# Two-layer hybrid trunk in fp32: wide GpSimd steps of layer 0, ple_proj and the gates moved to VectorE and ScalarE, gate inputs deferred by one half, ScalarE's table load moved ahead

## The chip, the cores and the metric

The kernel runs on one core of one Trainium2 chip. Its time is the device time of one execution in microseconds: 2993.09 us before, the median of 3 runs (2991.86 to 2994.93). One execution was profiled; it took 2989.8 us, and its span, from the first to the last record, is 2988.1 us.

## The reference

Two layers on 1024 tokens of 1024 features, all in fp32. Layer 0 mixes tokens by RWKV-7 (8 heads of 64) and by gated DeltaNet (4 heads of 128) side by side, layer 1 by softmax attention over bands of chunks. What both layers do around their mixer:

```python
for i in range(DEPTH):                       # DEPTH = 2
    h = rmsnorm(x, norm_mix_g[i])
    if i % 2 == 0:
        proj = h @ even_w_in[e]
        dh = token_shift(h) - h
        y_a, v_first = rwkv7_group(h, dh, ...)        # uses (h + dh*mu) @ w1 and the like: the LoRA products
        y_b = gdn_group(...)
        mix = jnp.concatenate([y_a, y_b], -1) @ even_w_out[e]
    else:
        mix = chunk_band_attention(h, attn_w_qkv[o], ...) @ attn_w_out[o]
    x = x + mix
    hf = rmsnorm(x, norm_ffn_g[i])
    x = x + jnp.square(jax.nn.relu(hf @ mlp_w1[i])) @ mlp_w2[i]
    x = x + rmsnorm(p[i] @ ple_w_proj[i], ple_norm_g[i]) * jax.nn.sigmoid(x @ ple_w_gate[i])
return x
```

The last line is the gated embedding. Its first factor needs only `p`, the second needs x after the MLP.

## The kernel before

Tensors lie with features on the 128 partitions and tokens along the row, in tiles of 128 x 512: eight feature tiles, each with two token halves (`hf`). Every fp32 product is three passes on TensorE: ScalarE rounds an operand to a high part (`whi`, or the first half of `xg`, `act`), VectorE subtracts it to get the low part (`wlo`), and high x high, high x low and low x high are summed in a PSUM bank (`mm3`, whose matmuls all carry line 180). `split_w` (L316 and L317) does this for weights, `split_scaled` (L362/363, or L365/366 with a norm's gain) for activations. Weights arrive by SyncE's queue (SP), are split, and are used once.

RMSNorm scales rows, so it is applied behind the products: squares are summed over the eight tiles into `acc`, `row_stats` (L388 and the small steps L294 to L304) sums that over partitions by one-column matmuls and takes the inverse root, `to_rows` spreads it over partitions, and each eviction multiplies by it.

*Order.* Lanes (Python generators for the RWKV heads, the DeltaNet heads, the projections, ple_proj and the first products of the out-projection) are interleaved by a planner, `run`, which takes the lane whose estimated time is smallest. Tile's scheduler then orders each engine's instructions anew by a simulated time line. So an edit in one place can move instructions of other engines nearby.

*The start* (`l0_in`, L591 on). The first x tiles come half by half: two by ScalarE's queue, the others by SP's (L610). Each is split and its squares taken on ScalarE (`square`, L688), and GpSimd adds them to `acc` (L690) for the first token half; for the second half VectorE does. The statistics wait for the eighth: `self.plan` runs `row_stats` when the second projected tile is done and `to_rows` at the third. `lora` (L711) multiplies raw LoRA weights by per-feature mixing factors on GpSimd (L722), splits the two results, and adds the two products on GpSimd (L732). In layer 0 GpSimd also does the triangular solver's small subtractions (L421 to L431, L461), and the solver (`iz`, `F`, `T`, `Z` tiles) copies on ScalarE.

*ple_proj* (L1720). For each of 8 feature tiles and 2 halves: 6 matmuls of p with the embedding's weights, an eviction times `hpleg` (half of the norm's gain, one number per partition) on VectorE (L1740), the square on ScalarE (L1742), its sum on GpSimd (L1744), and a store of the scaled tile to DRAM (`pnd`, L1745). At the end `row_stats`. In layer 0 it lies beside the last units of the mixer (753 to 807 us), in layer 1 beside the last attention heads (2125 to 2172 us). There ScalarE also scales queries and keys (L2006, L2008), takes the softmax's exponentials (L2073) and splits probabilities (L362).

*The gates* (`tail`, L1676 on). Eight output tiles with two halves each. A half is 24 matmuls (`dense`); then, in `ev_gate`: tanh on ScalarE into a scratch tile of a ring of four (L1680), the load of `pn` from DRAM (L1682), its multiplication by the row statistics `prs` on GpSimd (L1683), (tanh + 1) * pn on VectorE (L1684), x += that (L1685), and the store of x (L1687 or L1689). In layer 0 the new x is at once made layer 1's input: split (L1692), squared on ScalarE into another scratch tile (L1695), summed on GpSimd (L1696).

*The seam.* At the last gate tile `load_qkv` (L1917) loads and splits head pair 0's weights `wq` in places of old ring tiles. `attn_in` (L1925) then makes queries, keys and values of four blocks of 128 tokens per half, each in a PSUM bank of 24 matmuls of 128 x 384, which ScalarE (L1946, L1950) and VectorE (L1951) evict with the row factor `rscol`. Blocks 0 and 1 of pair 0 take the two banks `sn`, the others the two of the common ring:

```python
if pr == 0 and i < 2:
    ps = psm.tile([P, HB], F32, tag="sn", name="dps", bufs=2)[...]
else:
    ps = self.bank([P, 3, P])
```

## Time and profile before

| | |
|---|---|
| median of the runs | 2993.09 us (2991.86 to 2994.93) |
| profiled execution | 2989.8 us, span 2988.1 us |
| mean granted TensorE clock | 0.987 |
| busy: TensorE | 2917.3 us (98%) |
| busy: VectorE | 2100.8 us (70%) |
| busy: ScalarE | 1441.8 us (48%) |
| busy: GpSimd | 476.2 us (16%) |
| HBM | 283.54 MB read, 125.89 MB written, 137 GB/s |
| first gate eviction of layer 0 to its last | 1578 to 1659 us |

In the rows of the trace PE is TensorE's matmuls, PEld its weight loads, DVE VectorE, ACT ScalarE, POOL GpSimd, and SPq SyncE's queue of DMA issues. A timeline row gives start, duration, engine, line, operation, output<-input, type and count, and in brackets the idle time of that engine just before and what ended it. Rows such as "L1740 DVE ... 737/748/751" give the shortest, median and longest duration in ns of a group. The granted clock is TensorE's, 1.00 at full speed.

### The profile page before, as it was taken

Reading aid. Unit: us, or ns where it says so; the run is one execution under the profiler, and the core shown is the slowest. Engines: PE = TensorE matmul, PEld = TensorE weight load, DVE = VectorE, ACT = ScalarE, POOL = GpSimd, SP = SyncE. Lnnn points to the kernel's source line nnn. Section 1 sums busy time; section 2 is a strip of 40 time slices with the busy share of each in tenths; the row PEclk is TensorE's granted clock in tenths of the full one; section 3 lists DMA queues with packets and bytes.
Section 4 is the critical chain, followed back from the end, with each engine's and each line's share of the span. In section 5 each row is a group of like instructions: output and inputs, shape, how many; then the busy total and the mean of one; then the engine's idle time right before and its main releaser. Section 6 shows DMA issues by size and latency. Waiting matters only on the chain.

```text
span 2988.1 us, 46702 instructions
## 1 busy us (share of the span) xinstructions
PE 2917.3 (98%) x17190; PEld 2420.8 (81%) x17190; DVE 2100.8 (70%) x4137; ACT 1441.8 (48%) x2828; POOL 476.2 (16%) x947
## 2 busy tenths in 40 slices
PE   8999999999999999999999899999999999999999
PEld 6777778777777888888888899999888888888887
DVE  7665654645749777787886677676859677878883
ACT  4443432323427555544443466666747555544441
POOL 5442330433400000000004211111200000000002
PEclk9999999899999999999999999999999999999999
DMA  6534324232446444754433211110366444754423
GB/s 220 201 127 140 116 86 140 77 120 82 144 141 230 161 149 153 252 179 153 154 111 120 86 49 44 48 63 24 113 234 214 141 155 153 254 182 147 148 97 118
DMA packets 205157, 412.49 MB, mean 138 GB/s; under 512 B 46352, under 2 KB 48640, under 8 KB 204928
## 3 DMA queue, kind: packets, MB, share of 16 engines
q1 hardware_dynamic: 174112, 353.40, 35.8%
q10 hardware_dynamic: 30816, 56.11, 4.9%
q8 instruction: 135, 2.21, 0.3%
q14 instruction: 94, 0.77, 0.1%
HBM read 283.54 MB, written 125.89 MB: 137 GB/s over the span
## 4 chain that ended last, share of the span: by engine, by line
PE 78%; DVE 8%; DMA 6%; POOL 3%; ACT 3%; issue 2%; SPq 0%; ACTq 0%; POOLq 0%; DVEq 0%
PE dps L180 64%; PE ch L180 2%; PE po L180 2%; PE iz L180 1%; PE pt L195 1%; PE pm L180 1%; POOL subt L428 1%; POOL sub L430 1%; PE sn L180 1%; PE tp L180 1%; DVE act L1319 1%; PE py L180 1%; DMA late<-hd 1%; DMA Xp<-z 1%; PE pp L180 1%
## 5 line engine op out<-in xcount | busy, mean ns | idle before, releaser
L180 PE MATMUL dps<-r,act 128*128 128x512 f32 x3720 | 872.3, 392 | 0.4 <-DVE act L1319 0.4
L180 PEld LDWEIGHTS dps<-r,act 128*128 128x128 f32 x3720 | 698.5, 188 | 154.2 <-DVE act L1319 0.9
L180 PE MATMUL dps<-xg,whi 128*128 128x512 f32 x1248 | 419.1, 415 | 13.4 <-ACT whi L316 9.6
L180 PE MATMUL dps<-wq,act 128*128 128x384 f32 x1536 | 303.7, 342 | 8.6 <-ACT late L1680 4.3
L1683 POOL TENSOR_TENSOR pn<-pn,prs 128x512 f32<-128x512 f32 x32 | 45.7, 1431 | 1539.9 <-DVE xw L1586 713.3
L180 PEld LDWEIGHTS dps<-xg,whi 128*128 128x128 f32 x1248 | 227.3, 193 | 63.6 <-ACT whi L316 11.2
L180 PEld LDWEIGHTS dps<-wq,act 128*128 128x128 f32 x1536 | 264.8, 190 | 11.7 <-DVE vs L1951 4.8
L180 PE MATMUL dps<-xg,wlo 128*128 128x512 f32 x624 | 251.5, 404 | 4.6 <-DVE wlo L317 4.6
L1318 ACT CAST act<-act 128x512 fp32r<-128x512 f32 (+2 forms) x281 | 160.4, 600 | 150.3 <-PE dps L180 72.8
L1319 DVE TENSOR_TENSOR act<-act 128x512 fp32r<-128x512 f32 (+2 forms) x281 | 180.7, 670 | 6.7 <-ACT act L1318 6.5
L1318 ACT CAST act<-late 128x512 fp32r<-128x512 f32 x210 | 123.6, 620 | 110.3 <-PE dps L180 94.5
L180 PE MATMUL dps<-act 128*128 128x512 f32 x720 | 175.0, 391 | 1.5 <-DVE late L1440 1.5
L180 PE MATMUL dps<-late,act 128*128 128x512 f32 x672 | 166.7, 393 | 0.0
L1319 DVE TENSOR_TENSOR act<-late,act 128x512 fp32r<-128x512 f32 x210 | 138.7, 685 | 37.5 <-ACT act L1318 37.5
L180 PEld LDWEIGHTS dps<-act 128*128 128x128 f32 x720 | 134.9, 188 | 31.5 <-DVE late L1440 2.3
L180 PEld LDWEIGHTS dps<-late,act 128*128 128x128 f32 x672 | 126.0, 188 | 27.7
L180 PEld LDWEIGHTS dps<-xg,wlo 128*128 128x128 f32 x624 | 120.1, 193 | 34.2 <-DVE wlo L317 7.1
L180 PE MATMUL dps<-xw,act 128*128 128x512 f32 x576 | 145.9, 392 | 1.3 <-ACT act L1318 1.3
L1586 DVE TENSOR_TENSOR xw<-xw,dps 128x512 f32<-128x512 f32 x192 | 129.6, 679 | 21.6 <-PE dps L180 21.6
L180 PEld LDWEIGHTS dps<-xw,act 128*128 128x128 f32 x576 | 107.9, 188 | 25.4 <-ACT act L1318 1.7
L2073 ACT ACTIVATE pb<-pb,mx 128x640 f32<-128x640 f32 (+4 forms) x128 | 89.2, 697 | 51.8 <-DVE mx L2067 50.8
L180 PE MATMUL po<-ptile,vs 128*128 128x256 f32 (+1 forms) x576 | 98.5, 283 | 3.8 <-ACT ptile L362 1.4
(513 smaller groups left out, 5292.6 us busy)
## 6 DMA issues: line engine op xcount, KB each, us to landing
hb<-late ACTq DMA_DIRECT2D x196, 256.0 KB
act<-hb SPq DMA_DIRECT2D x158, 256.0 KB
late<-in_w SPq DMA_DIRECT2D x60, 512.0 KB
act<-in_w SPq DMA_DIRECT2D x112, 256.0 KB
braw<-hb SPq DMA_DIRECT2D x80, 256.0 KB
wd<-whi SPq DMA_DIRECT2D x28, 512.0 KB
wd<-wlo SPq DMA_DIRECT2D x28, 512.0 KB
whi<-wd SPq DMA_DIRECT2D x28, 512.0 KB
```

Of the source, the lines that this page charges most:

```text
L180: return self.begin(self.nc.tensor.matmul(out, lhsT, rhs, start=start, stop=stop, skip_group_check=again))
L195: return self.begin(self.nc.tensor.transpose(out, in_, ident))
L428: E.tensor_tensor(o, X[:, 0:i, i:i + 1].broadcast_to((NP, i, n)), Bq[:, i:i + 1, i + 1:16].broadcast_to((NP, i, n)), op=ALU.mult)
L430: E.tensor_tensor(X[:, 0:i, i + 1:16], X[:, 0:i, i + 1:16], o, op=ALU.add)
L1318: A.copy(hi, s)
L1319: V.tensor_tensor(lo, s, hi.bitcast(F32), op=ALU.subtract)
L1586: V.tensor_tensor(x[n][:, hs[hf]], x[n][:, hs[hf]], ps, op=ALU.add)
L1683: G.tensor_tensor(pn, pn, prs[:, sl], op=ALU.mult)
L2073: A.activation(S, S, AF.Exp, bias=mx[:, 1:2] if nf else mx[:, 0:1], scale=-1.0, accum_out=l)
```

## The change

1. Behind the second x load on ScalarE's queue a Tanh of one column of a constant tile is issued (`early`); the table that ScalarE needs is loaded for it.
2. The first half's square sums go from GpSimd to VectorE, and are written into the plan step of the second projected tile (`first_rows`), with `row_stats`.
3. `lora`: the 12 multiplications of raw weights and the 4 additions go from GpSimd to VectorE.
4. Gates, both layers: `pn` is loaded one half ahead (`load_ple`; the first before the gate loop) and multiplied by `prs` on VectorE at the end of a half's eviction, for the next half (`scale_ple`): 32 multiplications. In layer 0 the making of layer 1's input moves to `next_input`, which is called one half later (at the last tile at once), and its 14 sums go from GpSimd to VectorE.
5. `ple_proj`, both layers: the 32 evictions times `hpleg` go from VectorE to ScalarE, the 28 sums of squares from GpSimd to VectorE.
6. `attn_in`, pair 0: block 3 takes the bank `sf` of its own.

In all 97 wide operations leave GpSimd (952 instructions to 855), VectorE gets these 97 and gives 32, ScalarE gets 32 and the one-column Tanh; TensorE's matmuls and SP's DMAs are the same in number.

```diff
                         (nc.sync if k > 1 else nc.scalar).dma_start(out=xr, in_=a["x"][k, :, 0:HB])
+                        if k == 1:
+                            early = self.sm.tile([P, 4], F32, tag="rsc", name="early")
+                            nc.scalar.activation(early[:, 0:1], self.ones[:, 0:1], AF.Tanh)
...
-                        squares.append(lambda k=k, xr=xr: self.square(acc, xr, k == 0))
-                for f in squares:
-                    f()
+                        squares.append(lambda k=k, xr=xr: self.square(acc, xr, k == 0, nc.vector))
+                def first_rows():
+                    for f in squares:
+                        f()
+                    self.row_stats([acc], rsc)
...
-                    self.late, self.plan = [], {2: lambda: self.row_stats([acc], rsc), 3: ...}
+                    self.late, self.plan = [], {2: first_rows, 3: ...}
...
-                nc.gpsimd.tensor_tensor(wv[:, :, c0:c1], rv[:, :, c0:c1],
+                nc.vector.tensor_tensor(wv[:, :, c0:c1], rv[:, :, c0:c1],
...
-        nc.gpsimd.tensor_tensor(out, out, sb[:, 0:HB], op=ALU.add)
+        nc.vector.tensor_tensor(out, out, sb[:, 0:HB], op=ALU.add)
...
+            def load_ple():
+                if ple:
+                    n, hf = ple.pop(0)
+                    nc.sync.dma_start(out=pn2[:, hf], in_=self.pnd[n][:, hf, :])
+                    landed.append(hf)
+            def scale_ple():
+                if landed:
+                    hf = landed.pop(0)
+                    V.tensor_tensor(pn2[:, hf], pn2[:, hf], prs[:, hs[hf]], op=ALU.mult)
+            def next_input(n, hf):
+                sl = hs[hf]
+                if hf == 0:
+                    xg.append(place(F32R, tag="b" if n < 2 else "a"))
+                self.split_scaled(xg[n], x[n][:, sl], self.vec("mixg", 8 + n), sl)
+                if n:
+                    sq = scr()
+                    A.activation(sq, x[n][:, sl], AF.Square)
+                    V.tensor_tensor(accs[hf], accs[hf], sq, op=ALU.add)
+                else:
+                    A.activation(accs[hf], x[n][:, sl], AF.Square)
...
                     A.activation(sg, ps, AF.Tanh, scale=0.5)
-                    pn = pn2[:, hf]
-                    nc.sync.dma_start(out=pn, in_=self.pnd[n][:, hf, :])
-                    G.tensor_tensor(pn, pn, prs[:, sl], op=ALU.mult)
-                    V.scalar_tensor_tensor(sg, sg, 1.0, pn, op0=ALU.add, op1=ALU.mult)
+                    load_ple()
+                    V.scalar_tensor_tensor(sg, sg, 1.0, pn2[:, hf], op0=ALU.add, op1=ALU.mult)
                     V.tensor_tensor(x[n][:, sl], x[n][:, sl], sg, op=ALU.add)
...
+                    nc.sync.dma_start(out=a["out"][n, :, sl] if last else self.xd[n][:, sl], in_=x[n][:, sl])
+                    if not last:
+                        todo.append((n, hf))
+                        while len(todo) > (n < NK - 1):
+                            next_input(*todo.pop(0))
+                    scale_ple()
...
-                    nc.vector.tensor_scalar(t[:, hf, :], ps, self.dv["hpleg"][:, 8 * i + n:8 * i + n + 1], None, op0=ALU.mult)
+                    nc.scalar.activation(t[:, hf, :], ps, AF.Copy, scale=self.dv["hpleg"][:, 8 * i + n:8 * i + n + 1])
...
-                        nc.gpsimd.tensor_tensor(acc[:, hf, :], acc[:, hf, :], sq, op=ALU.add)
+                        nc.vector.tensor_tensor(acc[:, hf, :], acc[:, hf, :], sq, op=ALU.add)
...
-            if pr == 0 and i < 2:
-                ps = psm.tile([P, HB], F32, tag="sn", name="dps", bufs=2)[:, 0:3 * P].rearrange("p (a c) -> p a c", a=3)
+            if pr == 0 and i in (0, 1, 3):
+                tag, n = ("sn", 2) if i < 2 else ("sf", 1)
+                ps = psm.tile([P, HB], F32, tag=tag, name="dps", bufs=n)[:, 0:3 * P].rearrange("p (a c) -> p a c", a=3)
```

How the order moves is shown at three places. First VectorE at the kernel's start, before; `xg` is the split of x (L366), `wlo` a weight's low part, `ms` and `rsc` the row statistics:

```order
L366 SCALAR_TENSOR_TENSOR xg<-f,vecs,xg 128x512
L317 TENSOR_TENSOR wlo<-wraw,whi 128x512
L366 SCALAR_TENSOR_TENSOR xg<-f,vecs,xg 128x512 x6
L317 TENSOR_TENSOR wlo<-wraw,whi 128x1024 x2
L317 TENSOR_TENSOR wa_434<-wraw,wa_434 128x512
L388 TENSOR_SCALAR ms<-st 128x4
```

and the same place now, where lines carry the changed kernel's numbers (L695 is the sum of squares):

```order
L366 SCALAR_TENSOR_TENSOR xg<-f,vecs,xg 128x512 x2
L695 TENSOR_TENSOR acc<-acc,f 128x512
L366 SCALAR_TENSOR_TENSOR xg<-f,vecs,xg 128x512 x2
L695 TENSOR_TENSOR acc<-acc,f 128x512
L366 SCALAR_TENSOR_TENSOR xg<-f,vecs,xg 128x512
L695 TENSOR_TENSOR acc<-acc,f 128x512
L317 TENSOR_TENSOR wlo<-wraw,whi 128x1024
L695 TENSOR_TENSOR acc<-acc,f 128x512 x3
L317 TENSOR_TENSOR wlo<-wraw,whi 128x1024
L388 TENSOR_SCALAR ms<-st 128x4
```

The seven sums stand between the splits and the wide low parts: four ahead of the first wide `wlo`, three between the two, and the statistics follow directly.

Second VectorE at the last gates of layer 0, before; `late` is the scratch tile, `x` the residual tile, `act` its split, `wq` the attention's weights:

```order
L1684 SCALAR_TENSOR_TENSOR late<-late,pn 128x512
L1685 TENSOR_TENSOR x_12747<-x_12747,late 128x512
L366 SCALAR_TENSOR_TENSOR act<-x_12747,vecs,act 128x512
L1922 TENSOR_TENSOR wq_15706<-late,wq_15705 128x1024
L1684 SCALAR_TENSOR_TENSOR late<-late,pn 128x512
L1685 TENSOR_TENSOR x_12747<-x_12747,late 128x512
L366 SCALAR_TENSOR_TENSOR act<-x_12747,vecs,act 128x512
L1684 SCALAR_TENSOR_TENSOR late<-late,pn 128x512
```

and now (L1713 and L1714 are the gate's two steps, L1693 the scaling of `pn`, L1703 the sum of squares, L1946 the weights' split):

```order
L1713 SCALAR_TENSOR_TENSOR late<-late,pn 128x512
L1714 TENSOR_TENSOR x_12749<-x_12749,late 128x512
L366 SCALAR_TENSOR_TENSOR act<-x_12749,vecs,act 128x512
L1693 TENSOR_TENSOR pn<-pn,prs 128x512
L1703 TENSOR_TENSOR acc<-acc,late 128x512
L1946 TENSOR_TENSOR wq_15706<-late,wq_15705 128x1024
L1713 SCALAR_TENSOR_TENSOR late<-late,pn 128x512
L1714 TENSOR_TENSOR x_12749<-x_12749,late 128x512
L366 SCALAR_TENSOR_TENSOR act<-x_12749,vecs,act 128x512
```

Two steps join each half, the scaling and the sum. The names don't tell the halves of a tile apart, so the rows can't show whose split it is; it stands where it stood, behind the gate's two steps, and the weights' split ahead of the last three halves, as before.

Third ScalarE in ple_proj(1), before; `sq` is the square, `pb` are attention scores, `yr` and `pt` tiles that are split:

```order
L2076 ACTIVATE pb<-pb,rl 128x640
L2073 ACTIVATE pb,rl<-pb,mx 128x640
L1742 ACTIVATE sq<-dps 128x512
L2073 ACTIVATE pb,rl<-pb,mx 128x640
L2076 ACTIVATE pb<-pb,rl 128x640
L362 CAST act<-yr 128x512 x4
L2076 ACTIVATE pb<-pb,rl 128x640
L1742 ACTIVATE sq<-dps 128x512
```

and now (L1764 is the eviction times `hpleg`, L1766 the square, L2098 and L2101 the exponentials and their scaling):

```order
L1764 ACTIVATE act<-dps,d_hpleg 128x512
L2098 ACTIVATE pb,rl<-pb,mx 128x640
L1766 ACTIVATE sq<-dps 128x512
L2098 ACTIVATE pb,rl<-pb,mx 128x640
L1764 ACTIVATE act<-dps,d_hpleg 128x512
L362 CAST act<-yr 128x512 x4
L2101 ACTIVATE pb<-pb,rl 128x640
L1766 ACTIVATE sq<-dps 128x512
L2101 ACTIVATE pb<-pb,rl 128x640
L1764 ACTIVATE act<-dps,d_hpleg 128x512
```

The evictions stand among the exponentials, and a bank's two readers are now both on ScalarE, with other work between them.

19 lines of the change are left out of this document (5 added, 14 removed).

## The prediction

> **What bounds the kernel now.** I read the page's busy times first, then TensorE's waits, then a table of stages, and only then the timelines of the places that the change touches. The executed profile took 2989.8 us, 2988.1 of it span; the runs' median is 2993.09, so 3.3 us more. I make the sum against the profile and put the difference on the median.
>
> ```profile
> PE 2917.3 (98%) x17190; PEld 2420.8 (81%) x17190; DVE 2100.8 (70%) x4137; ACT 1441.8 (48%) x2828; POOL 476.2 (16%) x947
> ```
>
> TensorE is busy 2917.3 of 2988.1 us: 71 us is all that any other engine can give back as waits, and no matmul is removed. TensorE's waits by releaser (us in total, times, longest) tell who holds it:
>
> ```profile
> PE dps L180 <- ACT whi L316: 9.6, 5, 7.1
> PE dps L180 <- ACT late L1680: 4.3, 1, 4.3
> PE dps L180 <- DVE vs L1951: 3.7, 3, 2.2
> ```
>
> The first is mostly the start (7.1, the first matmul), the second and third are the seam between layer 0's gates and layer 1's first qkv products: all in the change's reach. A busy TensorE can also be a slow one. In the table by stages the columns are window, its length, busy time (and count) of PE, PEld, DVE, ACT, POOL, granted clock, DMA share, GB/s:
>
> ```profile
> 0.00:30.00 30.00, 21.08 (x85) 16.16 (x86) 14.25 (x26) 16.43 (x27) 23.15 (x85) 1.00 0.82 301
> 30.00:70.00 40.00, 36.96 (x166) 27.11 (x165) 34.61 (x73) 18.68 (x31) 14.87 (x18) 1.00 0.51 172
> 414.60:418.00 3.40, 3.40 (x19) 2.42 (x19) 2.58 (x8) 1.26 (x3) 1.34 (x5) 0.51 0.38 122
> 421.40:432.00 10.60, 9.98 (x49) 6.83 (x49) 4.87 (x9) 2.03 (x4) 5.87 (x14) 0.52 0.47 135
> 745.00:805.00 60.00, 55.70 (x504) 42.22 (x502) 50.68 (x105) 28.68 (x66) 30.14 (x43) 1.00 0.36 129
> 807.00:821.00 14.00, 13.45 (x60) 10.02 (x55) 8.28 (x21) 4.99 (x9) 3.79 (x10) 0.51 0.64 204
> 1650.20:1657.20 7.00, 5.28 (x17) 5.28 (x18) 4.83 (x5) 3.39 (x6) 3.95 (x3) 0.51 0.24 87
> 2124.00:2172.00 48.00, 44.31 (x269) 37.52 (x267) 43.70 (x115) 42.02 (x89) 20.23 (x15) 1.00 0.43 160
> ```
>
> Four rows stand at half clock. The stretch after the gates follows a wait of TensorE; those at 414.6 and 807 do not: TensorE is busy 3.40 of 3.40 and 13.45 of 14.00 us there, on the delta rule's small products. What half clock costs is half of its length: 7 us at half clock lose 3.5.
>
> **The start** (ScalarE's table, the squares' sums). Rows of ScalarE, GpSimd, VectorE and TensorE:
>
> ```profile
> 3.98 1.28 ACT L365 ACT_TABLE_LOAD   x1 [3.98 <-DMA vecs<-in_vecs]
> 7.13 1.22 PE L180 MATMUL dps<-xg,whi 128*128 128x512 f32 x2 [7.13 <-ACT whi L316]
> 8.39 0.72 ACT L365 ACTIVATE xg<-f,vecs 128x512 fp32r<-128x512 f32 x1 [0.17 <-DMA f<-in_x]
> 13.23 5.76 POOL L690 TENSOR_TENSOR acc<-acc,f 128x512 f32<-128x512 f32 x3
> 15.74 2.09 DVE L317 TENSOR_TENSOR wlo<-wraw,whi 128x1024 fp32r<-128x1024 f32 x1
> 17.89 0.50 PE L180 MATMUL dps<-xg,wlo 128*128 128x512 f32 x1 [1.03 <-DVE wlo L317]
> 422.00 1.23 DVE L317 TENSOR_TENSOR wlo<-wraw,whi 128x1024 fp32r<-128x1024 f32 x1 [3.15 <-ACT whi L316]
> L690 DVE TENSOR_TENSOR acc<-acc,xr x7: 671/680/830, 32.5 to 42.3; 128x512 f32<-128x512 f32 x7
> ```
>
> The table load waits for the vectors until 3.98, and takes 1.28. The early Tanh reads only a constant, so the load runs while ScalarE idles, and the first split, the first weight cast and the first matmul come up to 1.28 us earlier. But the third x tile lands at about 8.3 either way (the 8.39 row): of the 1.28 I count 0.7, with ends 0 and 1.28. The seven sums go from GpSimd (5.76/3 = 1.92 each) to VectorE (0.68). Beside GpSimd a wlo took 2.09, against the 1.23 that a 128x1024 wlo takes at 422.00, with GpSimd idle: 0.86 of the 1.03 wait at 17.89 goes. Against it, 7 x 0.68 = 4.8 us now stand in VectorE's own order, four sums among the splits and three, 2.0 us, between the two wide wlo's; it has 14.25 of 30 us busy and the splits wait for tiles, so I let the gaps hide them. I take **-1.5** for the start. Ends: -3 (both effects whole, and the statistics earlier) and +2 (the three sums, 2.0 us, in front of a wlo that is waited for).
>
> **The LoRA multiplies and adds.** In 30 to 70 us VectorE is 34.61 of 40 busy, so the eight 128x512 multiplies are not free there; what they buy is rows like these:
>
> ```profile
> 51.44 1.29 POOL L732 TENSOR_TENSOR f<-f,raw 128x512 f32<-128x512 f32 x1
> 51.56 1.20 DVE L783 TENSOR_SCALAR gs_ab<-gs_ab 128x16 f32<-128x16 f32 x1
> 53.01 0.17 DVE L783 TENSOR_SCALAR gs_ab<-gs_ab 128x16 f32<-128x16 f32 x1
> 54.58 0.50 PE L180 MATMUL dps<-xg,wlo 128*128 128x512 f32 x1 [0.98 <-DVE wlo L317]
> 418.99 1.89 POOL L722 TENSOR_TENSOR wraw<-lraw,d_omul 128x1024 f32<-128x1024 f32 x1 [1.97 <-DMA lraw<-in_lora]
> 422.02 1.22 PE L180 MATMUL dps<-xg,whi 128*128 128x512 f32 x2 [1.16 <-ACT whi L316]
> ```
>
> The 16-element operation beside the GpSimd add takes 1.20 in place of 0.17, and the wlo behind it is late by that 1.03; the add itself on VectorE costs 0.68, so 0.35 is won at such a place and 0.68 lost where nothing was stretched. First half: **-0.5**, ends -2 and +2 (four wide places each way). At 419 the multiply of 1.89 stands in TensorE's way (the 1.16 wait); on VectorE it takes about 1.23, a wlo's size, and 0.7 goes. The half clock from 421.4 may begin one 3.4 us grain later or not: **-1.0**, ends -4 and +1.
>
> **ple_proj(0).** VectorE gives 16 evictions and takes 14 adds; GpSimd gives the adds:
>
> ```profile
> L1740 DVE TENSOR_SCALAR xg<-dps,d_hpleg x16: 737/748/751, 753.5 to 800.9; 128x512 f32<-128x512 f32 x16
> L1744 POOL TENSOR_TENSOR xg<-xg,xs x14: 1249/1273/1717, 760.6 to 804.3; 128x512 f32<-128x512 f32 x14
> 787.40 1.67 DVE L297 TENSOR_TENSOR rsw<-fr 128x4 f32<-128x4 f32 x1
> 790.63 0.62 PE L195 MATMUL pp<-ident,fr 128*128 128x128 f32 x4 [1.35 <-DVE fr L304]
> 805.57 1.05 PE L180 MATMUL dps<-ones,xg 128*128 128x1 f32 x8 [0.47 <-POOL xg L1744]
> ```
>
> VectorE, 50.68 of 60, sheds 16 x 0.748 - 14 x 0.68 = 2.4 us, and its 4-element steps (1.67 here) are no longer stretched, so the 1.35 wait goes. ScalarE, 28.68 of 60, has room for 16 evictions. The last statistics come 1.27 - 0.68 = 0.6 earlier plus whatever queued on GpSimd. The half clock that follows (13.6 us, from 807) may shrink by one grain of 3.4, worth 1.7. I take 1.35 + 1.7 = **-3.0**. Ends: -8 (the stretch gone as well) and +2 (ScalarE's longer evictions in front of the solver's copies).
>
> **Layer 0's gates and the seam.** One half-tile of a gate is 24 matmuls; 258 take 58.65 us, so a half takes 58.65 x 24 / 258 = 5.46.
>
> ```profile
> 1588.96 58.65 PE L180 MATMUL dps<-r,late 128*128 128x512 f32 x258
> 1641.88 0.68 DVE L1684 SCALAR_TENSOR_TENSOR late<-late,pn 128x512 f32<-128x512 f32 x1
> 1646.26 1.63 POOL L1683 TENSOR_TENSOR pn<-pn,prs 128x512 f32<-128x512 f32 x1 [6.52 <-DMA pn<-pnd]
> 1646.68 1.77 DVE L1684 SCALAR_TENSOR_TENSOR late<-late,pn 128x512 f32<-128x512 f32 x1
> 1650.90 0.75 DVE L366 SCALAR_TENSOR_TENSOR act<-x,vecs,act 128x512 fp32r<-128x512 f32 x1 [0.79 <-ACT act L365]
> 1651.29 0.57 ACT L1680 ACTIVATE late<-dps 128x512 f32<-128x512 f32 x1
> 1651.92 15.13 PE L180 MATMUL dps<-wq,act 128*128 128x384 f32 x72 [4.31 <-ACT late L1680]
> ```
>
> The last evictions run late: each tanh waits for its scratch tile, that for the sum on GpSimd, and VectorE's steps take 1.77 in place of 0.68 beside GpSimd. TensorE then stands 4.31 us for a bank. After the change a half costs VectorE four steps of 0.68 and a split's 0.75, 3.5 us, plus here and there a weight's lo part of 1.23: under 5.46. So the evictions keep up, and the scaled pn is ready a step ahead. The load's lateness is nothing new: it was issued at the tanh, and now stands one half earlier on SP's queue, behind stores of x. What is late next is the last tile's input, tanh, two steps, and both halves of a split, 0.57 + 0.68 + 0.68 + 0.72 + 0.75 = 3.4 us after the last gate matmul; but the first qkv block takes the other token half's tiles, ready 5.46 us before. I take the 4.31 as gone, with the half clock behind it (7.0 us at 0.51, which lose 3.4), and the 2.2 for L1951 too, since the fourth block of head pair 0 has a bank of its own and the fifth finds one free: **-9.9**. Ends: -11 and -5 (the store that the wq ring waits for, or a late tanh, keeps 2 to 3 us and with them the clock's fall).
>
> The Trainium skill's "TensorE: Matmul & The Clock Gate" (Part 1) says that the clock halves after an idle window of about 3.4 us. The 4.31 us wait fits; by that rule alone, 414.6 and 807 would not be at half clock, and no shift in layer 0 could lengthen or shorten such stretches: the first two grains above would fall out and the gain be some 2 us smaller. The trace's 3.40 of 3.40 busy at clock 0.51 speaks against the rule in that form, so I keep them.
>
> **ple_proj(1)**, beside attention. ScalarE has 42.02 of 48 busy. An eviction scaled by a pointer is not in the trace at 128x512 from PSUM; the nearest rows are 64x512:
>
> ```profile
> 2103.45 0.68 ACT L2006 ACTIVATE F<-dps,d_qg 64x512 fp32r<-64x512 f32 x1
> 2104.14 0.68 ACT L2008 ACTIVATE F<-dps,d_qg 64x512 fp32r<-64x512 f32 x1
> ```
>
> They start 0.69 apart: 16 x 0.69 = 11.0, and 42.02 + 11.0 = 53.0 us of work for 48. VectorE falls from 43.70 to about 41. So ScalarE takes VectorE's place as the fullest engine, 5.0 us over; keeping today's idle 6 as well, 11 over. TensorE's slack and ScalarE's idle after 2172 take part of it: **+3**, ends -1 (VectorE's relief wins) and +11. By the Trainium skill's "ScalarE: Activation LUTs" (What ACT_TABLE_LOAD costs) a pointer adds about 93 ns and neighbours overlap by as much, some 0.61 each, an estimate of 9.8 in place of 11.0; the trace's spacing does not show that overlap.
>
> **Layer 1's gates**: 0. They end the kernel, their pn was ready in time, and the 16 multiplies of 0.68 fall into halves of 5.46; ends -0.5 and +1.5.
>
> Sum: -1.5 - 0.5 - 1.0 - 3.0 - 9.9 + 3.0 = **-12.9**, on 2993.09 gives **2980**. What a measurement of this kernel can tell from no change is 0.2%, 6 us.
>
> **Rivals.** *The seam keeps its wait* (16%): another tile of the scratch or weight ring holds the last evictions, and the seam gives 3 in place of 9.9: -12.9 + 6.9 = -6, 2987. For it: the multiply of pn at 1646.26 had sat 6.52 us for its load, so SP's queue, on which the loads still stand behind stores, is late too. Against: the loads go a half earlier, and VectorE's 3.5 us a half are well under 5.46. *ScalarE binds in ple_proj(1)* (10%): its upper end, +11, makes the sum -4.9, 2988. For: 53 of 48. *Half clock gets rarer* (14%): the half-clock rows at 414, 421 and 807 alone are 28 us, costing 14; if those stretches in layer 0 go, -12.9 - 10 = -23, 2970. *Slower: half clock gets commoner* (8%). The scheduler writes layer 0's order anew, VectorE is its fullest engine (34.61 of 40, 50.68 of 60) and gets 23 wide operations before 500 us (7 sums, 12 multiplies, 4 adds), so dense products can wait behind small ones for longer. Each further stretch like that at 807 costs 7; three of them cost 21, +8, 3001. It brings the sum to nothing from 13 us of loss, two stretches, and past the bound of a measurement from 19, three. That the change doesn't do what it says can be left out: the order of the changed kernel has no wide GpSimd step left in the gates.
>
> **Numbers.** My own case has 52%, 2974 to 2987. Range 2968 to 2992: about 8% below it (the clock's best case), 12% above. Faster: 52 + 14 + half of 16 and of 10, 0.79; same: the other halves, 0.13; slower 0.08.
>
> **What would show it.** Right: no wait over 1 us at the end of layer 0's gates, no half clock behind them, the step that now is L1684 at 0.69 throughout, the first matmul before 6.5 us, and ScalarE at over 48 us in a ple_proj(1) that lasts some 3 us longer. Wrong: a wait of 3 us or more after the last gate matmul under another name, ple_proj(1) longer by over 6 us, or time at half clock in layer 0 that differs by more than 20 us.

## The result and the profile after

The changed kernel takes 2988.81 us, the median of its runs (2981.68 to 2998.41). Its ratio to the kernel before, whose median beside it was 2995.43, is 0.9983 (95% interval 0.9975 to 0.9990): 5 us faster, where 13 were forecast. A later series of both on another chip gave 0.9995 (0.9984 to 1.0007), which is no difference that can be told from none. The profiled execution has a span of 2986.6 us. Runs of one and the same kernel lie up to 10 us (the changed one) and 12 us (before) from their median, and the profile of before, at 2989.8, is 5.6 us below the median of this series, so differences of single profiles are good to a few microseconds only.

Busy times from the page of the changed kernel, then some of TensorE's waits there (us in total, times, longest):

```profile
PE 2921.5 (98%) x17190; PEld 2425.9 (81%) x17190; DVE 2100.4 (70%) x4202; ACT 1459.0 (49%) x2861; POOL 342.4 (11%) x850
```

```profile
PE iz L180 <- ACT T L455: 5.2, 3, 2.9
PE iz L180 <- ACT TZ L505: 3.4, 1, 3.4
...
PE dps L180 <- ACT act L365: 2.2, 1, 2.2
```

GpSimd lost 134 us of work, as meant. The waits for `late` (4.3 before, 0.4 now) and `vs` (3.7 before, 1.5 now) are gone from the head of the list. In their place stand the solver's first step (L455, 5.2 where before had 3.7) and its copy (L505, 3.4, where before had none), in layer 0, where the change only moved work from GpSimd to other engines. At the gates' end 2.2 us remain, under another name (`act`).

The start, from the timelines of ScalarE and TensorE:

```profile
1.72 1.28 ACT L613 ACT_TABLE_LOAD   x1 [1.72 <-PEq L2233]
4.18 0.72 ACT L365 ACTIVATE xg<-f,vecs 128x512 fp32r<-128x512 f32 x1 [0.97 <-DMA f<-in_x]
6.81 1.22 PE L180 MATMUL dps<-xg,whi 128*128 128x512 f32 x2 [6.81 <-ACT whi L316]
16.91 0.50 PE L180 MATMUL dps<-xg,wlo 128*128 128x512 f32 x1 [0.53 <-DVE wlo L317]
34.49 0.74 PE L180 MATMUL dps<-xg,whi 128*128 128x512 f32 x2 [1.82 <-ACT whi L316]
```

The table is in place 2.26 us earlier and the first split 1.10 earlier, but the first matmul only 0.32: it waits for the weight's cast, which starts at 6.14 after 0.72 us of waiting for its load. The wait for `wlo` is 0.53 in place of 1.03. At 34.49 there is a new one of 1.82.

The table by stages, first the changed kernel, then the kernel before; columns as above (length, busy PE, PEld, DVE, ACT, POOL, granted clock, DMA share, GB/s):

```profile
20.00:100.00 80.00, 77.48 (x356) 60.71 (x355) 56.37 (x121) 31.45 (x55) 16.61 (x32) 0.96 0.61 218
35.40:42.30 6.90, 6.20 (x17) 4.84 (x17) 6.30 (x13) 4.07 (x8) 0.00 (x0) 0.51 0.58 192
100.00:250.00 150.00, 141.18 (x1375) 108.93 (x1374) 92.95 (x216) 62.02 (x146) 60.95 (x154) 0.95 0.43 149
1650.00:1664.00 14.00, 11.38 (x55) 10.74 (x54) 8.12 (x12) 5.01 (x8) 4.92 (x8) 0.88 0.52 188
2124.00:2175.00 51.00, 44.83 (x255) 37.22 (x254) 40.28 (x104) 48.00 (x98) 1.29 (x1) 0.97 0.41 143
```

```profile
20.00:100.00 80.00, 76.96 (x362) 59.35 (x362) 54.44 (x111) 31.56 (x55) 38.01 (x58) 1.00 0.59 210
100.00:250.00 150.00, 142.97 (x1419) 109.60 (x1418) 95.39 (x223) 63.14 (x151) 57.45 (x142) 1.00 0.45 155
```

Two things can be read from such a row: TensorE's idle time (length less PE busy) and what the clock took (length times one less the clock). In 100 to 250 us before had 7.0 idle and nothing lost to the clock; after has 8.8 idle and 0.05 x 150 = 7.5 lost. In 20 to 100 us the clock took 3.2, about what the stretch at 35.4 behind the new wait lost. The half clock behind the gates is down to 0.12 x 14 = 1.7.

Where the time went I measured by equal matmuls: how much later or earlier the n-th matmul starts in a trace than in that of before, and how that difference grows over a stretch. Below it is called the shift. It counts matmuls of every size, and small products can change places with wide ones; at the times below a count of the 128x512 ones alone gives the same within 0.5 us in nearly all traces, and at 2200 us within 1.

### The profile page after: what moved, and what is told of

Same layout as the page of the kernel before. It is cut to its first block, busy times and chain, and to the rows that moved or that the text cites. A ratio compares the mean times of both kernels' runs of the same rounds, so it can differ in the third digit from the quotient of the medians.

```text
span 2986.6 us, 46646 instructions
## 1 busy us (share of the span) xinstructions
PE 2921.5 (98%) x17190; PEld 2425.9 (81%) x17190; DVE 2100.4 (70%) x4202; ACT 1459.0 (49%) x2861; POOL 342.4 (11%) x850
## 4 chain that ended last, share of the span: by engine, by line
PE 80%; DVE 7%; DMA 6%; ACT 3%; POOL 2%; issue 2%; SPq 0%; ACTq 0%; DVEq 0%; POOLq 0%
PE dps L180 65%; PE ch L180 3%; PE po L180 2%; PE iz L180 1%; PE pt L195 1%; PE pm L180 1%; PE sn L180 1%; PE tp L180 1%; DMA pn<-pnd 1%; POOL subt L428 1%; POOL sub L430 1%; PE py L180 1%; DVE act L1324 1%; DMA Xp<-z 1%; PE sf L180 1%
## 5 line engine op out<-in xcount | busy, mean ns | idle before, releaser
L2098 ACT ACTIVATE pb<-pb,mx 128x640 f32<-128x640 f32 (+4 forms) x128 | 89.4, 699 | 53.1 <-DVE mx L2092 52.2
L1323 ACT CAST r<-act 128x512 fp32r<-128x512 f32 x126 | 76.0, 617 | 52.5 <-PE dps L180 38.1
```

Of the source, the lines that this page charges most:

```text
L1323: A.copy(hi, s)
L2098: A.activation(S, S, AF.Exp, bias=mx[:, 1:2] if nf else mx[:, 0:1], scale=-1.0, accum_out=l)
```

## The experiments

Each kernel is the changed one with the edit shown; the parts' numbers are those of the change.

**Layer 0's parts 1 to 3 undone, and the gates alone.** In the first, the early Tanh is out, and the square sums and the LoRA multiplications and additions are back on GpSimd; the second undoes `ple_proj` (part 5) too.

```diff
-                            nc.scalar.activation(early[:, 0:1], self.ones[:, 0:1], AF.Tanh)
-                        squares.append(lambda k=k, xr=xr: self.square(acc, xr, k == 0, nc.vector))
+                        squares.append(lambda k=k, xr=xr: self.square(acc, xr, k == 0))
-                nc.vector.tensor_tensor(wv[:, :, c0:c1], rv[:, :, c0:c1],
+                nc.gpsimd.tensor_tensor(wv[:, :, c0:c1], rv[:, :, c0:c1],
-        nc.vector.tensor_tensor(out, out, sb[:, 0:HB], op=ALU.add)
+        nc.gpsimd.tensor_tensor(out, out, sb[:, 0:HB], op=ALU.add)
```

> The changed kernel with parts 1 to 3 undone (no early Tanh, the first half's sums and all LoRA steps on GpSimd); gates, ple_proj and the extra bank stay. Theory (by place): the changed kernel loses at 142 us because ScalarE's new order puts the solver's first step, which waits for a DMA, ahead of a copy that TensorE needs (3.4 us of wait and 6.8 us at half clock), and gains 5.6 near 420; with parts 1 to 3 undone both go, the kernel is level with the one before at 725 us, and ends 4 to 5 us faster than before up to the gates, 6 to 9 us faster in all after the seam's gain and ple_proj(1)'s loss. Rival (by chance): the clock's half-speed stretches in layer 0 fall by the phase of the run and not by the order; then this run differs from the kernel before by several us at 200 us although the order there is the same, and its time is that of the changed kernel within 2 us.

> Only part 4 and part 6: the gates without GpSimd and the extra bank, all else as before. Theory: everything up to 1500 us is as before, the seam gives about 5 us in place of the 9.9 forecast, because evictions still end about 6 us after TensorE's last gate matmul; the whole kernel is 4 to 6 us faster than before. Rival: the gain of the changed kernel came from ple_proj(0) alone and the seam's gain is eaten by the pn multiplies on VectorE; then this kernel is within 2 us of before.

Without parts 1 to 3: 2985.3 us, 0.9964 (0.9951 to 0.9976). The gates alone: 2989.8 us, 0.9987 (0.9976 to 0.9998). So parts 1 to 3, forecast at -3, cost 0.0019 x 2993 = 5.7 us. The gates gave 5 us in the shift of both (1500 to 1700 us: -5.4 and -5.2), half of the forecast.

**Layer 1's `ple_proj` back** on VectorE and GpSimd.

```diff
-                    nc.scalar.activation(t[:, hf, :], ps, AF.Copy, scale=...)
+                    if i:
+                        nc.vector.tensor_scalar(t[:, hf, :], ps, ..., None, op0=ALU.mult)
...
-                        nc.vector.tensor_tensor(acc[:, hf, :], acc[:, hf, :], sq, op=ALU.add)
+                        (nc.gpsimd if i else nc.vector).tensor_tensor(acc[:, hf, :], acc[:, hf, :], sq, op=ALU.add)
```

> The changed kernel with ple_proj of layer 1 as before (eviction on VectorE, sums on GpSimd); layer 0's ple_proj stays changed. Theory: ScalarE is the limit in ple_proj(1), so the 3.1 us lost between 2125 and 2175 come back: the waits for the square and for the probabilities (2.1 and 2.4 us) go, and the time falls by 3 us against the changed kernel, 0.9972 to 0.9977 of the kernel before. Rival: the loss there is a shift of order and clock, not ScalarE's load; then the stretch still takes over 2 us more than before.

2985.74 us, 0.9976 (0.9963 to 0.9989), 2 us under the changed kernel, a difference that the two intervals alone don't separate. The stage with the edit, to set against the 2124 row of the changed kernel:

```profile
2124.00:2172.00 48.00, 44.41 (x265) 38.16 (x264) 42.49 (x112) 41.54 (x85) 20.25 (x15) 0.96 0.45 161
```

ScalarE has 41.5 of 48 here, and 48.00 of 51 in the change. From 2100 to 2200 us the shift grows by 2.5 on average (1.6 to 3.6) in the 13 traces with the new `ple_proj(1)`, and by 0.4 on average (-1.35 to +2.0) in the six with the old one; by the 128x512 matmuls alone 3.3 and 0.5.

**The scaling of `pn` behind the gate's first step.** The multiplication by `prs` moves from the load to the tile, so that nothing on VectorE waits for the load ahead of its time.

```diff
-                    V.tensor_tensor(pn2[:, hf], pn2[:, hf], prs[:, hs[hf]], op=ALU.mult)
...
                     V.scalar_tensor_tensor(sg, sg, 1.0, pn2[:, hf], op0=ALU.add, op1=ALU.mult)
+                    V.tensor_tensor(sg, sg, prs[:, sl], op=ALU.mult)
```

> The changed kernel with the gates' factor prs multiplied on VectorE into the tanh's tile, right behind the step (tanh + 1) * pn, in place of into pn ahead of it; loads, counts and all else stay. Theory: in the changed kernel VectorE stands 11.8 us in the gates of layer 0 in front of the scaling of pn, for its DMA, because the scheduler put that step ahead of the next half's first step; without it the last evictions come 3 to 6 us earlier, the wait of 2.2 us after the last gate matmul and the half clock behind it (1.7) go, and the seam gains another 3 to 4 us, less 0.7 at the kernel's end where the chain is one step longer: 2 to 4 us faster than the changed kernel. Rival: the evictions are late because VectorE and ScalarE wait for each other around the splits of the weights; then the idle time in front of the scaling turns up in front of other steps, the wait after the last gate matmul stays within 0.7 us, and the time within 1 us.

2987.61 us, 0.9969 (0.9955 to 0.9982), 4 us under the changed kernel. Why it helps is seen at the gates' last halves in the changed kernel, timelines of VectorE, SP and ScalarE (L1693 scales `pn`, L1713 is the gate's first step, L1687 the load, L365 the split of x):

```profile
1641.16 0.68 DVE L1713 SCALAR_TENSOR_TENSOR late<-late,pn 128x512 f32<-128x512 f32 x1
1641.87 0.32 SPq L1687 DMA_DIRECT2D pn<-pnd  x1
1645.46 0.69 DVE L1693 TENSOR_TENSOR pn<-pn,prs 128x512 f32<-128x512 f32 x1 [1.35 <-DMA pn<-pnd]
1647.81 0.69 DVE L1713 SCALAR_TENSOR_TENSOR late<-late,pn 128x512 f32<-128x512 f32 x1
1649.26 0.72 ACT L365 ACTIVATE act<-x,vecs 128x512 fp32r<-128x512 f32 x1 [3.98 <-DVE x L1714]
```

The load into a `pn` buffer can be issued only when the step that read it is done (1641.16 + 0.68, issue at 1641.87), and lands 3.6 us later. The scheduler has put the scaling for that load ahead of the other half's gate step, and the engine goes in order: VectorE idles for a load that nobody needs yet, and the gate step stands behind. ScalarE hangs on it too: its split L365 waits 3.98 us for the x that the step makes, and the next tanh, which frees TensorE's bank, stands behind that split and starts at 1650.41. VectorE's groups over the gates, the changed kernel from 1578 to 1660 us, then with the edit from 1584 to 1666 us (busy time, mean ns, idle time before and its releaser):

```profile
L1713 DVE SCALAR_TENSOR_TENSOR late<-late,pn 128x512 f32<-128x512 f32 x16 | 10.9, 686 | 5.5 <-ACT late L1711 5.5
L1693 DVE TENSOR_TENSOR pn<-pn,prs 128x512 f32<-128x512 f32 x14 | 9.7, 692 | 11.8 <-DMA pn<-pnd 11.8
```

```profile
L1714 DVE TENSOR_TENSOR late<-late,prs 128x512 f32<-128x512 f32 x16 | 11.1, 691 | 0.4
L1713 DVE SCALAR_TENSOR_TENSOR late<-late,pn 128x512 f32<-128x512 f32 x16 | 11.0, 688 | 9.4 <-ACT late L1711 9.4
```

The 11.8 us of idleness for the load are gone; VectorE now waits for the tanh, as it should (9.4 in place of 5.5). A third `pn` buffer, with which the load need not wait for that step, was not tried. The seam as a whole, from the first tanh of the gates to the first statistics matmul behind layer 1's first products, before, changed, and with the edit (timelines of ScalarE and TensorE):

```profile
1577.71 0.60 ACT L1680 ACTIVATE late<-dps 128x512 f32<-128x512 f32 x1 [5.77 <-PE dps L180]
1666.88 1.84 PE L180 MATMUL st<-ones,acc 128*128 128x1 f32 x16
```

```profile
1580.40 1.09 ACT L1711 ACTIVATE late<-dps 128x512 f32<-128x512 f32 x2 [5.31 <-PE dps L180]
1648.55 3.83 PE L180 MATMUL dps<-wq,act 128*128 128x384 f32 x21
1654.62 0.62 PE L180 MATMUL dps<-wq,act 128*128 128x384 f32 x2 [2.24 <-ACT act L365]
1665.82 1.84 PE L180 MATMUL st<-ones,acc 128*128 128x1 f32 x16
```

```profile
1583.87 0.60 ACT L1711 ACTIVATE late<-dps 128x512 f32<-128x512 f32 x1 [5.77 <-PE dps L180]
1653.61 12.67 PE L180 MATMUL dps<-wq,act 128*128 128x384 f32 x72
1666.11 1.84 PE L180 MATMUL st<-ones,acc 128*128 128x1 f32 x16
```

They take 89.17, 85.42 and 82.24 us: the change wins 3.75 here, the edit 6.93, with its 72 products in one piece at full speed. With the 2.2 that were forecast for `vs` behind it that is 9.1 of the forecast's 9.9: over 1500 to 1700 us the shift with the edit is -9.4, and -9.1 to -9.4 in the four runs below that have it too; in the 14 traces without it, it is -3.3 to -6.5, -4.8 on average.

**Parts 1 to 3 split.** The LoRA operations back on GpSimd (part 3 undone), and the LoRA operations alone on VectorE (parts 1 and 2 undone).

```diff
-                nc.vector.tensor_tensor(wv[:, :, c0:c1], rv[:, :, c0:c1],
+                nc.gpsimd.tensor_tensor(wv[:, :, c0:c1], rv[:, :, c0:c1],
```

> The changed kernel with part 3 alone undone (LoRA's multiplies and adds on GpSimd); early Tanh and the first sums stay changed. Parts 1 to 3 together cost about 5 us (ratio 0.9964 without them, 0.9983 with them). Theory: VectorE is the fullest engine of layer 0 and the LoRA's multiplies make it late, so this kernel gets most of that back: 0.9965 to 0.9975 of the kernel before. Rival: the cost comes with parts 1 and 2, which pull the statistics 17 matmuls forward and reorder everything behind; then this kernel stays at 0.998.

> The changed kernel with parts 1 and 2 undone (no early Tanh, the first half's sums on GpSimd); LoRA stays on VectorE. Theory (LoRA's load on VectorE costs): this kernel stays near 0.998 of the kernel before. Rival (the start reorders layer 0): it comes to 0.9965 to 0.9975.

3000.88 us, 1.0020 (1.0007 to 1.0033), and 3006.22 us, 1.0035 (1.0022 to 1.0048): either half of the three is worse than all of them (0.9983) or none (0.9964). The parts don't add up, which points to the order that the scheduler makes of them. In both kernels one wait of TensorE stands out, of about 10 us near 140 us; TensorE's timeline of the first, and the row of the second's waits (in total, times, longest):

```profile
146.25 1.07 PE L180 MATMUL iz<-X,T 32*32 32x32 f32 x32 [9.24 <-DVE T L479]
```

```profile
PE iz L180 <- DVE T L479: 10.6, 2, 10.2
```

ScalarE there: the changed kernel, the kernel with the LoRA operations alone, and the one without parts 1 to 3:

```profile
144.59 0.35 ACT L455 ACTIVATE T<-Xp,half 128x64 f32<-128x64 f32 x1 [7.13 <-DMA Xp<-z]
144.85 0.56 ACT L505 COPY TZ<-iz 64x512 f32<-64x512 f32 x1
```

```profile
148.95 0.35 ACT L455 ACTIVATE T<-Xp,half 128x64 f32<-128x64 f32 x1 [10.25 <-DMA Xp<-z]
```

```profile
141.56 0.58 ACT L505 COPY TZ<-iz 64x512 f32<-64x512 f32 x1 [1.82 <-PE iz L195]
```

It is the gates' pattern again: L455, the first step of the next solver unit, waits for its load and stands ahead of a copy of the unit before that TensorE waits for: L505 in the changed kernel (3.4 us), L479, half of which is ScalarE's, in the two kernels above. Without parts 1 to 3 the copy comes first. The theory from here was that this order costs the 5.7 us.

**The solver's first step on GpSimd**, so that ScalarE isn't held.

```diff
-        A.activation(T1, curT, AF.Copy, scale=m1)
+        G.tensor_scalar(T1, curT, m1, None, op0=ALU.mult)
```

> The changed kernel with the solver's first step (T, line 455, which waits for the DMA of Xp) on GpSimd in place of ScalarE, in all 16 calls. Theory: no wait for the copy TZ at 142 us, no half clock at 144, so 6 to 7 us less at 225 us than in the changed kernel, and 4 to 7 us less in all, unless GpSimd's step is late for TensorE elsewhere (0.44 us in place of 0.35 each). Rival (by chance): half clock falls elsewhere in 125 to 225 us and the time stays within 2 us of the changed kernel.

2989.27 us, 0.9988 (0.9974 to 1.0002). The wait is gone and the shift at 250 us is 8 us better (-1.8 against +6.2), but a 2.8 us wait came at 419.7 and, beside the stretch at half clock near 595 us that the changed kernel has too, a second one of 14 us at 623. The time is that of the changed kernel, so this run doesn't decide.

**The order alone.** A rule to the scheduler, without a wait in the program: this step not ahead of the previous unit's copy; put on the changed kernel and on that with the LoRA operations alone.

```diff
-        A.activation(T1, curT, AF.Copy, scale=m1)
+        t1 = A.activation(T1, curT, AF.Copy, scale=m1)
+        self.tc.add_manual_dep(t1.ins, self.tz.ins.name, ..., reason="order")
...
-        out(TZ[lo], pz)
+        self.tz = out(TZ[lo], pz)
```

> The changed kernel with one rule for the scheduler: the solver's first step T of a unit (line 455, waits for the DMA of Xp) may not stand ahead of the copy TZ of the unit before on ScalarE. No instruction is added, no wait but the order. Theory: the wait of 3.4 us at 142 us and the half clock behind it (3.4) go, 5 to 7 us less than the changed kernel, 0.996 to 0.9968 of the kernel before, as without parts 1 to 3 (0.9964). Rival (the cost of parts 1 to 3 is the load that they put on VectorE): the wait goes, but the time stays within 2 us of the changed kernel, 0.998.

> The kernel with LoRA alone of parts 1 to 3 (e7, 1.0035) with the same rule of order. Theory: its wait of 10.2 us at 140 us goes, with the half clock of 13.7 us behind it (6.8), so it falls by 12 to 17 us, to 0.998 or below. Rival: VectorE's added load made it slow, and it stays above 1.001.

2988.15 us, 0.9981 (0.9971 to 0.9990), and 2998.74 us, 1.0015 (1.0003 to 1.0027). The second fell by 6 us of the 12 to 17 expected, the first not at all. The order is as wanted. In the second the wait near 140 us is gone, yet by 250 us its shift is 20 us, with the rule as without it. In the first the next unit's wait takes the place (TensorE's timeline):

```profile
182.25 0.29 PE L180 MATMUL iz<-T,N 32*32 32x16 f32 x10 [2.89 <-ACT F L502]
```

So that wait alone doesn't carry the cost, and the theory fell.

**Three of them again, on one chip**: the change, the change without parts 1 to 3, and the change with the rule.

> The changed kernel itself, on one chip with e14 and e15. Both theories: 0.9975 to 0.999 of the kernel before, and a profile that is 5 to 8 us behind the kernel before between 100 and 250 us.

> Parts 1 to 3 undone, the kernel of e1, on the same chip. Theory (parts 1 to 3 cost by what they do to the order between 100 and 250 us): 3 to 6 us less than e13, and its profile no more than 4 us behind the kernel before at 250 us. Rival (the difference of e1 and the changed kernel was that of two chips): within 2 us of e13.

> The kernel of e9 (the changed kernel with the rule of order) on the same chip. Theory (the one wait of 3.4 us at 142 us is most of the cost): within 2 us of e14. Rival (other waits of the new order, for the next unit's T, take its place): within 2 us of e13.

2990.23 us, 0.9995 (0.9984 to 1.0007); 2982.12 us, 0.9972 (0.9961 to 0.9983); 2987.36 us, 0.9992 (0.9981 to 1.0003). Parts 1 to 3 cost 0.0023 x 2990 = 6.9 us on one chip, and the rule again gives nothing. The stages of the first two:

```profile
20.00:100.00 80.00, 77.46 (x362) 60.61 (x361) 57.26 (x122) 32.55 (x56) 17.04 (x34) 0.98 0.63 224
100.00:250.00 150.00, 139.80 (x1329) 107.98 (x1330) 91.10 (x212) 58.81 (x137) 60.72 (x152) 0.92 0.42 143
250.00:850.00 600.00, 585.28 (x5097) 454.15 (x5096) 345.34 (x889) 224.77 (x546) 169.76 (x504) 0.95 0.33 109
```

```profile
20.00:100.00 80.00, 77.11 (x363) 59.45 (x362) 55.45 (x110) 31.49 (x55) 37.64 (x59) 1.00 0.61 213
100.00:250.00 150.00, 144.15 (x1395) 110.58 (x1393) 94.71 (x223) 62.49 (x150) 55.70 (x139) 0.97 0.45 155
250.00:850.00 600.00, 586.06 (x5042) 453.64 (x5042) 339.40 (x875) 221.69 (x536) 179.60 (x512) 0.94 0.33 109
```

From 100 to 250 us parts 1 to 3 add 10.2 - 5.85 = 4.35 of idle time and 12 - 4.5 = 7.5 of lost clock; 66 matmuls fewer were done by its end. From 20 to 100: -0.35 and +1.6; from 250 to 850: +0.8 and -6 (a clock of two figures is good to 3 us over such a length). Together some 8, against 6.9 measured. But the place is less sure than the sum, for single profiles differ there by as much: from 100 to 250 us the shift grows by 5.9 and 11.0 in the two profiles of the changed kernel, and by 7.1 and 1.4 in the two of the kernel with the rule, whose time is the same; and the kernel without parts 1 to 3, which runs the operations of before there in almost the same order, loses 4.5 to the clock (0.97) where the profile of before lost nothing. From 400 to 450 us a part comes back: -4.1 on average in the 11 traces with all three parts, +0.6 in the five with none.

**SP's queue.** The second suspect: at 78 us the store `scr` and its loads `subb`, which feed the solver, stand behind a 512 KB load and weights' stores; SP before and in the changed kernel:

```profile
77.00 0.32 SPq L409 DMA_DIRECT2D scr<-N  x1
...
80.15 3.58 SPq L413 DMA_DIRECT2D subb<-scr  x8
```

```profile
77.39 0.43 SPq L310 DMA_DIRECT2D wraw<-in_w_in  x1
78.35 0.55 SPq L409 DMA_DIRECT2D scr<-N  x1
...
84.55 4.34 SPq L413 DMA_DIRECT2D subb<-scr  x8
```

The loads are issued 6.2 us after the store in place of 3.15. The rule lets `scr` go ahead of what the scheduler had put in front; the second kernel has both rules.

```diff
-        nc.sync.dma_start(out=raw, in_=src)
+        self.behind(nc.sync.dma_start(out=raw, in_=src), 0, 4)
...
-                nc.sync.dma_start(out=d, in_=z.bitcast(F32))
+                self.behind(nc.sync.dma_start(out=d, in_=z.bitcast(F32)), 1, 4)
```

> The changed kernel with one rule of order on SyncE's queue: the store of the first solver's matrices (scr) stands ahead of the fourth half-megabyte store of weights and of the fifth load behind it, as in the kernel before; nothing else is changed. Theory: in the changed kernel scr is issued behind one load and two stores more and lands 6.2 us after its issue in place of 3.2, so GpSimd's solver starts 5 us later and everything that hangs on its result is later; with the rule, subb's loads are issued near 80 us in place of 84, the first T stands near 110 in place of 115, and the time falls by 4 to 7 us against the changed kernel, to 0.9970 to 0.998. Rival: the order on ScalarE (T ahead of TZ) or VectorE's load costs the rest, and the time stays within 2 us of the changed kernel's although T comes earlier.

> The changed kernel with both rules of order: scr first on SyncE's queue, and T not ahead of TZ on ScalarE. Theory: level with the kernel without parts 1 to 3 (0.9972 and 0.9964 in two runs) or up to 3 us below it, since VectorE's and ScalarE's gains of parts 1 to 3 stay. Rival: no lower than e9 and e15 (0.9981, 0.9992).

2990.27 us, 0.9988 (0.9978 to 0.9997), and 2987.5 us, 0.9982 (0.9970 to 0.9994). `subb` starts at 79.7, as early as before the change, and the time stays that of the changed kernel. This isn't the cause either. The stretch in the first of the two:

```profile
100.00:250.00 150.00, 141.48 (x1386) 109.70 (x1385) 93.05 (x217) 61.91 (x148) 57.87 (x146) 0.95 0.43 147
```

Idle time (8.5) and clock (0.95) are those of the changed kernel's first profile (8.8 and 0.95).

**The parts that pay, together.** Parts 1 to 3 undone, layer 1's `ple_proj` back, the scaling behind; made twice. And the same two mendings with parts 1 to 3 kept, under the one rule and under both.

> Parts 1 to 3 undone, layer 1's ple_proj as before, and the scaling of pn behind the gate's first step: the parts that gained, with the seam's remaining wait taken away. Theory: the gains add, 5.5 (parts 1 to 3) + 2 (ple_proj of layer 1) + 3 (seam) on top of the changed kernel, 14 to 17 us less than before, 0.9945 to 0.9955. Rival: the places are not independent (a stretch at half clock comes back elsewhere), and it ends no lower than with parts 1 to 3 undone, 0.996.

> The kernel of e8 once more, on the chip of the runs above, for the comparison with e11 and for a second profile: the 37 us at half clock from 620 us in the profile of e8 are put down to one run. Theory: no such stretch here, 10 to 16 us less in the profiled run than in e8's, and 0.9935 to 0.995 of the kernel before. Rival: the stretch belongs to the kernel and comes again.

> The changed kernel with the rule of order, ple_proj of layer 1 as before, and the scaling of pn behind the gate's first step; parts 1 to 3 stay changed. Theory: all forecast gains in layer 0 without its new waits, so level with or 1 to 3 us below the kernel without parts 1 to 3 (e8, e12): 0.993 to 0.995. Rival: parts 1 to 3 cost even in a good order, and it is 3 us or more slower than that kernel.

> All parts of the change but layer 1's ple_proj, the scaling of pn behind the gate's first step, and both rules of order. Theory: 2 to 5 us below e11 (0.9954), so 0.9935 to 0.995, level with the kernel without parts 1 to 3 (e8, e12: 0.9942, 0.9940) or below. Rival: as e11.

2976.06 us, 0.9942 (0.9920 to 0.9963), and 2976.07 us, 0.9940 (0.9921 to 0.9960): some 17.5 us faster than before, and nearly 13 faster than the change. With parts 1 to 3 kept: 2978.16 us, 0.9954 (0.9939 to 0.9969), and 2980.96 us, 0.9961 (0.9946 to 0.9975), by the ratios 4 and 6 us slower than without them, though the intervals overlap. The first of the four had one execution of 2994.71, the profiled one, with five others from 2969.65 to 2978.02; it holds this row, behind a 3.34 us wait:

```profile
617.00:660.00 43.00, 39.66 (x254) 28.38 (x252) 10.38 (x27) 6.47 (x20) 11.47 (x40) 0.56 0.22 69
```

At 0.56 of 43 us the clock took 19. The second profile of the same code has no such stretch: where the clock falls differs from one execution to the next.

## Why the prediction was wrong

The direction held in the first series and 2988.8 lies in the range, but 13 us were forecast and 5 came, and the second series can't tell the change from none. Two terms failed, the seam's and that of layer 0's parts 1 to 3; the other three came out near.

- **The seam, forecast -9.9, measured about -5** (-3.3 to -6.5 in the traces). The step that failed is "So the evictions keep up, and the scaled pn is ready a step ahead". VectorE's load per half was right (3.5 of 5.46, and L1713 at 0.68 to 0.70 throughout), but I took a step that is issued early to be one that is done early. It was put in front of the step that counts, and waits for a load that can't be issued until the buffer is free. So the tiles of the first qkv block, which the prediction had ready 5.46 us before, were waited for: "no wait over 1 us" came out as 2.24, and the clock behind it as 0.88. With the scaling behind the step the same part gives -9.1 to -9.4: its price was right, the order wrong. The rival "the seam keeps its wait" is the nearest to what happened, with VectorE's order in place of the rings as its reason; the late load of `pn` that it named was the right sign.
- **Layer 0's parts 1 to 3, forecast -3.0 in sum, measured +5.7 and +6.9.** The start came in part: at 20 us the shift is -0.8 to -1.3 in the 11 traces with all three parts (forecast -1.5), though "the first matmul before 6.5 us" came at 6.81. The first half of `lora` did not come: at 100 us the shift is -0.7 on average (+0.4 to -2.3), where -2.0 were forecast, and in the changed kernel's profile the new wait of 1.82 and the half clock behind it stand between. The second half gave more than its -1.0: from 400 to 450 us -4.1 on average. What was missing is a stretch that none of these operations stands in, 100 to 250 us: there the shift grows by 5.5 to 11.2 in the four traces with parts 1 to 3 and nothing done to the order, and by 1.1 to 3.8 in the five without them, some 5.6 us less on average. The step that failed is the cover, "I let the gaps hide them": the sum priced each operation where it stands and put the rest of the changed order at nothing. The rival "half clock gets commoner", at 8%, named the mechanism; between the two profiles of one chip it took 9 us in the clock and 4 in waits up to 250 us, without turning the whole slower. The sign of 20 us more at half clock came out at the threshold: against the profile of before, the changed kernel's first profile lost 3.2 + 7.5 us more to the clock up to 250 us, some 21 us at half clock.
- **`ple_proj(0)`, forecast -3.0**: from 725 to 1500 us, where no other part stands, the shift is -3.9 on average in the 11 traces with parts 1 to 3 (-6.4 in the four without) and -1.5 in the one kernel with the old version; some -2.4 in the changed kernel. Near, as far as one trace of the old version can tell.
- **`ple_proj(1)`, forecast +3**: +2.5 against +0.4, so 2.1, or 2.8 by the wide matmuls. Right, with ScalarE at 48.00 of 51. The price of one eviction was too high, though, in the changed kernel's timeline of ScalarE:

```profile
2152.54 0.67 ACT L1764 ACTIVATE act<-dps,d_hpleg 128x512 f32<-128x512 f32 x1
2153.11 0.58 ACT L1766 ACTIVATE sq<-dps 128x512 f32<-128x512 f32 x1
```

  The next operation starts 0.57 later, not 0.69. The figure of the Trainium skill's "ScalarE: Activation LUTs" (What ACT_TABLE_LOAD costs), an estimate of some 0.61 each, was the nearer one: neighbours do overlap here.
- **Layer 1's gates, forecast 0**: from 2850 to 2900 us +0.1 to +0.8 in all traces, and nothing more behind. Right.

Stage by stage the two profiles of the changed kernel read, against that of before: to 100 us +0.3 and -0.8, to 250 us +5.9 and +11.0, to 725 us -3.0 and -5.2, to 1500 us -3.3 and -4.4, to 1700 us -3.5 and -4.8, from 2100 to 2200 us +2.6 and +2.7, the rest -0.5 and +0.5. That is -1.5 and -1.0 in all, against a profile of before that lies 5.6 and 0.8 us below the medians of the two series.

What stays open is which part of the changed order costs the 6 to 7 us. That parts 1 to 3 cost as much is shown, twice on the whole kernel. That it is lost from 100 to 250 us, as idle time and clock, is what most profiles show, but no run isolates it: with the rules of order the shift there was smaller (1.3 to 7.1 in six traces), and the changed kernel's time stayed. The two orders that stood out (L455 ahead of L505 on ScalarE, `scr` behind a load on SP) were mended singly and together without a gain. The rival on record with the rule, that the load on VectorE is the cost, came out as it was worded: the wait went and the time stayed. Against it stands that VectorE is busy for less from 100 to 250 us with parts 1 to 3 (92.95 and 91.10 us) than without (94.71), so it isn't shown either. That a denser run of small products would keep the clock up was not tested.

## What to carry to other kernels

A step that waits for a load belongs behind the work that is ready, and on an in-order engine its place is part of its price: read in the order what stands behind the wait, and when the load's buffer comes free. Price an edit also where it isn't made: under a scheduler, moving operations at 10, 50 and 420 us rewrote the order from 100 to 250 us as well, and the parts cost 6 to 7 us where 3 were to be gained. Test the parts of a change singly and in pairs; here three parts undone, half of another undone, and one mended gave 17.5 us in place of 5.

## What the runs showed of the hardware

- The clock fell behind a short wait: at 35.4 us to 0.51 for some 6.9 us, behind a wait of 1.82 and with TensorE busy for 6.20 of it. The Trainium skill's "TensorE: Matmul & The Clock Gate" (Part 1) has it fall after an idle window of about 3.4 us; the trace here shows it behind a shorter one, so the page's rule isn't the whole of it.
- One execution lost 19 us to the clock in one stretch at 617 us that another of the same code didn't have; the runs of the changed kernel lie from 2981.68 to 2998.41. Under 6 us, several series were needed to tell two kernels apart.
- From the issue of a store to DRAM to that of the loads that need it passed 3.15 us before the change, and 6.2 in the changed kernel, where a 512 KB load had been issued 1 us ahead on the same queue (77.00 to 80.15, 78.35 to 84.55).
